# First modulation: order of the weight and table loads, and of matvecs (in halves) and weight products

## Chip, cores and metric

The kernel runs on one core of a Trainium2 chip. The metric is the device time of one execution in microseconds (us); of several executions the median is given. Engines: TensorE (PE; PEld is its load of the stationary operand), VectorE (DVE), ScalarE (ACT), GpSimd (POOL) and SyncE (SP), which here only issues DMAs.

## What is computed

The reference runs two blocks on 256 tokens of 1024 features (`x`), with a second stream of 256 tokens (`ctx`) in the first block. Only the start of the first block matters here: a modulation from a conditioning vector, then one product for queries, keys, values and more.

```
for l in range(DEPTH):
    mod_x = (silu_c @ w_mod[l] + b_mod[l])[:, None, :]
    mod_c = (silu_cc @ w_mod[l] + b_mod[l])[None, None, :]
    sh1, sc1, g1, sh2, sc2, g2 = jnp.split(mod_x, 6, axis=-1)
    ...
    px = modulate(x, sh1, sc1) @ w_in[l]      # x * (1 + sc1) + sh1
    pc = modulate(ctx, csh1, csc1) @ w_in[l]
    qx, kx, vx, ux, gbx, gcx, fx = split_proj(px)
```

Everything behind that (attention, convolution, a Fourier mix, MLPs, in the second block a state space layer and another attention) is the same work in both kernels.

## The kernel before

The program is one stream of instructions for each engine, in the order in which the Python code emits them; an engine works strictly in that order and waits on semaphores. Python generators are "lanes" of work, and each `next(lane)` emits its next piece on all the engines that it needs. Writing those calls in another order is all it takes to change the schedule.

Weights come as units of 512 rows by 512 columns (1 MB, `raw`, five buffers). `build_plan` (line 337) lists them in the order of loading; `load_upto(n)` (238) emits the loads of the first n on SyncE's queue, and `done_with` (252) lets the next one follow when a unit has been used. For a product in pieces of 128 x 1024, ScalarE casts the weights to `whi` (line 266) and VectorE subtracts to `wlo` (line 277); `gemm` (284) does three matmuls for each tile: `whi` with the high part of the data, `wlo` with the high part, `whi` with the low part (lines 306 to 308 where tokens come out on the lanes).

The stage in question begins the program:

- The conditioning vectors `crow` and a table (`const0`: identity, the matrix `sum4`, and `selq`) are loaded, turned, and become silu(c) in `cs1` (lines 438 to 521). Bias vectors and others come in rows (`vrow`) and are turned by `trans_vec` (523); rows 3 (state space parameters) and `ldr` follow at once (530 to 535).
- The modulation that the first product needs (shift and scale, 2048 columns) comes in four quarters q = 0 to 3, two units each. `gemv` (546) multiplies silu(c) with the two units of a quarter by 4 matmuls each (`gv`, line 556), VectorE transposes the result (line 562), PE sums it with `sum4` (`g`, line 566), VectorE adds the bias (line 945, with line 946: "VectorE's sums" below).
- `mod_split` (line 760 on) then makes the modulated row tiles 2 q and 2 q + 1: ScalarE the high part `mh` (line 768), VectorE the whole `m` (769) and the low part `ml` (777), for each row tile first the 256 tokens of `x` and then those of `ctx`.
- `x` and `ctx` come in two halves of features (`load_x`), turned by PE (`transpose_x`, line 930).
- The v product (lane `gv` in `first0`, 96 matmuls) takes the row tiles in four pieces; piece p needs the modulation of quarter q = p. Each `next(gv)` emits half a piece: 12 matmuls. The first half makes the tokens of `x`, the second those of `ctx`.
- The lane `flow` prepares parameters of the state space layer: steps of some twenty small VectorE operations on 128 x 32, at four places of this stage.

`first0` (line 1704) writes that order out by hand. For q = 1 to 3 it emits both halves of the matvec of quarter q with VectorE's transposition; half a piece of the v product for quarter q - 1; `g` with the sums; the other half piece; `mod_split`; a step of `flow`. The last piece (24 matmuls) and then the q and k product (lines 310 to 312) follow.

Of the kernel before, what the change touches and what calls it, by code (L numbers as in the profile page):

```python
# [51 lines left out]
def _constants():  # L52
    """Tables that depend on shapes alone: name -> [128, n]."""
# [34 lines left out]
_GROUPS = (("ident", "sum4", "selq"), ("cos", "sin", "cs64"), ("c256", "s256"), ("hd2", "selh", "mask"))  # L88
# [15 lines left out]
def program(ctx: ExitStack, tc: tile.TileContext, A, out, taps=None):  # L104
# [27 lines left out]
    class Slots:  # L132
        """[128, 256] tiles, two of them in a slot."""
# [25 lines left out]
    def weave(main, *lanes):  # L159
        """For every step of main one of each lane; the rest of the lanes follows."""  # L160
        for _ in main:
            pump()
            for f in lanes:
                next(f, None)
        for f in lanes:
            run(f)

    def mix(order, *lanes):
        """Steps of the lanes in this order, and then the rest of them, those of the first last."""
        for i in order:  # L170
            f = lanes[int(i)]
            if callable(f):
                f()
            else:
                next(f, None)
        for g in (*lanes[1:], lanes[0]):
            if g is not None and not callable(g):
                run(g)
# [19 lines left out]
    class Unit:  # L198
        """Four row tiles by 512 columns of a matrix."""
# [13 lines left out]
    class Job:  # L213
        """All of a product's weights, 1024 rows by 512 columns, in four pieces: two row tiles of all columns
        where the other operand comes piece by piece, or else four row tiles of half the columns."""
# [40 lines left out]
    def split_weights(n, need=None):  # L256
        """Of the first n pieces what float32r holds of the weights; of the first need (all but one) the rest too."""
# [26 lines left out]
    def gemm(key, *passes, tok=False, nm=4):  # L284
        """For each pass (hi, lo, n, evac): evac(i, product) for nm tiles of 128 output features (tokens if tok).
        Products of 256 columns come two at a time."""
# [36 lines left out]
    def over2(t):  # L323
        """A [128, 256] factor for two row tiles."""
        return t.rearrange("p (o n) -> p o n", o=1).to_broadcast([128, 2, 256])
# [4 lines left out]
    def parts2(t, ps):  # L330
        """For each of two products its place in t."""
# [99 lines left out]
    C = {}  # L431

    def constants(i, tag, eng):
        t = const.tile([128, max(_CW[1], _CW[3]) if i else _CW[0]], F32, name=f"cst{i}", tag=tag)
# [4 lines left out]
    SP.dma_start(crow[0:8], A["c"].rearrange("b (k p) -> (b k) p", p=128))  # L439
    S.dma_start(crow[8:16], A["c_ctx"].rearrange("(k p) -> k p", p=128))  # L440
    S.dma_start(crow[16:24], A["c_2"].rearrange("b (k p) -> (b k) p", p=128))
    constants(0, "cst0", SP)
# [56 lines left out]
    G.dma_start(lam_in, A["diff_lambda"].rearrange("(o l) f d -> o (l f d)", o=1).to_broadcast([128, 512]))  # L499
# [32 lines left out]
    V.tensor_copy(ldr, ld.rearrange("k (g o) -> k g o", o=1).to_broadcast([32, 2, 64]))  # L532
    trans_vec(3)
    dt = const.tile([128, 32], F32, name="dt")
    transposed(dt, ldr.rearrange("k g p -> k (g p)"), 32)

# [5 lines left out]
    def fourths(t, q):  # L542
        """Of every 128 columns those that belong on the lanes of quadrant q."""
        return t.rearrange("p (i c) -> p i c", c=128)[:, :, 32 * q:32 * q + 32]

    def gemv(units, out_, wait=False, halves=False):
        """out_(p8): p8[:, i, s] = silu(c, c_ctx, c_2)[s] @ w[:, 128 i : 128 i + 128], feature on the lane."""
# [23 lines left out]
    def fillers():  # L571
        """Steps, three for each of the modulations that are left to TensorE."""
# [19 lines left out]
    def gemv_lanes(groups, lag=4):  # L592
        """The same with the products summed over row tiles on a vector engine, in small steps."""
# [59 lines left out]
    def rsqrt_steps(dst, v, n):  # L653
        """dst = 1 / sqrt(v): a first guess, then a step of second and one of third order."""
# [25 lines left out]
    # x and ctx, feature on the lane, two row tiles side by side  # L680
# [4 lines left out]
    class Stats:  # L685
        """Sums over the features of XT[s] and of their squares, tokens in four quadrants."""
# [4 lines left out]
        def add(self, n=1):  # L691
            """The next n row tiles are there."""
# [34 lines left out]
        def small_ln(self):  # L727
            """Steps: 1 / deviation and -mean / deviation, both over D."""
# [34 lines left out]
    def mod_split(parts, start=False):  # L763
        """Steps: hi + lo = src * sc + sh, by lane, for each of the parts."""
# [14 lines left out]
    def mod_split2(hl, src, k, gp, sh):  # L779
        """The same for the row tiles k and k + 1, src and each of hl side by side."""  # L780
# [8 lines left out]
    class Tiles:  # L789
        """[128, 256] row tiles, two side by side in a slot."""  # L790
# [10 lines left out]
    class Course:  # L801
        """A norm in two lanes: sums, factors and quotients, and what becomes of those, by pairs of row tiles."""
# [33 lines left out]
    class Norm:  # L836
        """Layer norm of XT[s] in place; split modulated parts into the columns of hl.
        Gain and bias for XT are keep: at once, or later if there are modulated parts."""
# [35 lines left out]
    def needing(g, key, *courses):  # L874
        """The product g, a pass for each of the courses, which keep ahead of it."""
# [36 lines left out]
    def mod_of(g, b, sc, sh):  # L912
        """Gain and bias of the modulated layer norm."""
# [23 lines left out]
    def first_mod(q):  # L937
        """Steps: the modulated row tiles 2 q and 2 q + 1."""
# [8 lines left out]
        yield from gemv(mq[q], out_)  # L947
# [6 lines left out]
    def attention(l, heads, q, k, v, streams, sink):  # L954
        """Differential attention in steps; sink(h, outputs [e, tokens]) for every head."""
# [4 lines left out]
        def operands(h):  # L960
            """Steps: what float32r holds of q and k, and next to it, on the other half of the rows, what is left:
            q as it is beside its rest, k's rest beside k."""
# [130 lines left out]
    def layer(l, mh, ml, first, ns, last=None):  # L1093
        """first(evacuations): steps of the products up to q, k and v."""
# [5 lines left out]
        def rope(t, n, outs=None):  # L1100
            """For n heads side by side, in place or into outs."""
# [117 lines left out]
        def residual(stats, gate, j, tw_=tw):  # L1219
            """Evacuation of a product into XT for the columns of the streams tw_."""  # L1220
# [93 lines left out]
    def cross(order, g, courses, *lanes, streams=1):  # L1314
        """Products g and, between them, norms of what the first of them makes."""
# [89 lines left out]
    def s5_prep():  # L1405
# [32 lines left out]
        # turns of 4, 8, ... 128 tokens  # L1438
# [9 lines left out]
        # the powers 1 to 4 of a token's factor, and the factors of B and C  # L1448
# [3 lines left out]
        def times(re, im, a, b, n):  # L1452
            """re + i im = a * b, for n columns of pairs."""
# [24 lines left out]
    def over(t, p0, np_, n, lead=None):  # L1478
        """[128, np_ pairs] of a [128, 32] tile, for each of n columns (and of lead planes)."""
# [5 lines left out]
    def s5_turns():  # L1485
        """Turns of every step, and the decay of four tokens."""
# [24 lines left out]
    def turn_all(dst, src, P, Q, p0):  # L1511
        """Steps: dst = src times each of the factors; [128, n, 2, 4, 16] and [128, 2, 4, 16]."""
# [9 lines left out]
    def s5_group(a):  # L1522
        """Steps: C and B of four pairs of groups, turned by 0 to 3 tokens (C) and by 0 to 4 (B)."""
# [30 lines left out]
    def s5_prepare(a, i, mats):  # L1554
        """Steps: the factors of two pairs' matrices, apart for each group."""
# [642 lines left out]
```

## Time and profile before

| | us |
|---|---|
| three runs | 1398.65, 1407.0, 1410.64 |
| median | 1407.0 |
| span of the profiled execution, first to last instruction | 1406.5 |
| PE busy in it | 1331.4 |
| VectorE busy in it | 1017.6 |
| ScalarE busy in it | 619.4 |

The profiled execution's own time is not listed apart; its span lies 0.5 us below the median of the runs. Rows of the timeline give the start of an instruction (or of a few of the same kind in a row, x4), its duration, and in brackets how long its engine had been idle and what ended that.

### The profile page before, as it was taken

What the parts mean: (1) busy time and instruction counts of PE and PEld (TensorE: products, weight loads), DVE (VectorE), ACT (ScalarE), POOL (GpSimd) and SP (SyncE); (2) the same over time, 40 slices, a digit from 0 to 9 for tenths busy, and PEclk for the clock granted to TensorE, in tenths of its full rate; (3) what the DMA queues carried; (4) which work ended last, traced back from release to release, by engine and by line L of the source; (5) the groups of instructions that cost most, each with busy time, mean ns of one, the idle gap of its engine ahead of it and who ended that gap; (6) DMA issues with size and microseconds to landing.
All of it is one profiled execution on the core that took longest, in us unless ns stands there. A gap on an engine that the chain in (4) does not pass through costs nothing.

```text
span 1406.5 us, 23747 instructions
## 1 busy us (share of the span) xinstructions
PE 1331.4 (95%) x9118; PEld 1143.0 (81%) x9118; DVE 1017.6 (72%) x2087; ACT 619.4 (44%) x1237; POOL 281.8 (20%) x532
## 2 busy tenths in 40 slices
PE   5899999999999999999999889999989899999998
PEld 3676666997888788888877779999977799879888
DVE  4778755588977767667948877788675577777875
ACT  2424443275023140233545548667646024565552
POOL 4042100001111011110213415666430222002000
PEclk8999999999999999999999989999998689999999
DMA  9725445115566747461336455776796657544241
GB/s 332 241 76 171 165 163 194 61 61 190 200 212 236 269 150 269 153 237 61 114 120 230 135 183 167 241 242 212 246 349 238 211 200 244 210 150 155 88 150 31
DMA packets 160514, 258.69 MB, mean 184 GB/s; under 512 B 29152, under 2 KB 54064, under 8 KB 160400
## 3 DMA queue, kind: packets, MB, share of 16 engines
q1 hardware_dynamic: 138912, 233.15, 48.9%
q0 software_dynamic: 8528, 22.39, 4.5%
q10 hardware_dynamic: 12960, 1.63, 0.8%
q8 instruction: 72, 1.18, 0.3%
q14 instruction: 42, 0.34, 0.1%
HBM read 240.33 MB, written 16.81 MB: 183 GB/s over the span
## 4 chain that ended last, share of the span: by engine, by line
PE 36%; DVE 7%; ACT 3%; DMA 3%; issue 1%; SPq 0%; ACTq 0%; DVEq 0%
PE mm L310 8%; PE mm L311 8%; PE mm L312 8%; DVE wlo L277 1%; DMA ud<-u 1%; PE mm L307 1%; PE mm L308 1%; PE mm L306 1%; PE pi L1599 1%; PE bc L749 1%; DMA cn<-in_a_C_im_dram 1%; ACT s L2104 1%; PE py L1914 1%; PE py L1916 1%; PE py L1915 1%
## 5 line engine op out<-in xcount | busy, mean ns | idle before, releaser
L310 PE MATMUL mm<-mh,whi 128*128 128x256 f32 (+1 forms) x1344 | 430.4, 320 | 1.3 <-ACT r L1267 1.0
L312 PE MATMUL mm<-mh,wlo 128*128 128x256 f32 (+1 forms) x1344 | 421.3, 313 | 2.0 <-DVE wlo L277 1.9
L311 PE MATMUL mm<-ml,whi 128*128 128x256 f32 (+1 forms) x1344 | 421.0, 313 | 0.9 <-DVE ml L787 0.6
L266 ACT CAST whi<-raw 128x1024 fp32r<-128x1024 f32 x226 | 234.3, 1048 | 321.7 <-PE mm L311 251.9
L277 DVE TENSOR_TENSOR wlo<-raw,whi 128x1024 fp32r<-128x1024 f32 x256 | 309.3, 1222 | 31.0 <-ACT whi L266 28.6
L310 PEld LDWEIGHTS mm<-mh,whi 128*128 128x128 f32 x1344 | 259.5, 193 | 27.6 <-issue 10.0
L312 PEld LDWEIGHTS mm<-mh,wlo 128*128 128x128 f32 x1344 | 259.0, 193 | 17.3 <-DVE wlo L277 3.2
L311 PEld LDWEIGHTS mm<-ml,whi 128*128 128x128 f32 x1344 | 259.5, 193 | 15.2 <-DVE ml L787 1.5
L310 PE MATMUL mm<-hh,whi 128*128 128x256 f32 (+1 forms) x544 | 179.6, 330 | 0.4 <-DVE xT L1226 0.4
L312 PE MATMUL mm<-hh,wlo 128*128 128x256 f32 (+1 forms) x544 | 177.8, 327 | 1.8 <-DVE wlo L277 1.8
L311 PE MATMUL mm<-hl,whi 128*128 128x256 f32 (+1 forms) x544 | 177.7, 327 | 0.0
L268 POOL TENSOR_SCALAR whi<-raw 128x1024 fp32r<-128x1024 f32 x30 | 42.9, 1430 | 421.4 <-PE mm L311 356.6
L633 DVE SCALAR_TENSOR_TENSOR ga<-raw,ce,ga 128x512 f32<-128x512 f32 x154 | 120.1, 801 | 3.5 <-DMA raw<-in_a_mod_w_dram 1.0
L310 PEld LDWEIGHTS mm<-hh,whi 128*128 128x128 f32 x544 | 103.4, 190 | 10.9 <-issue 2.0
L312 PEld LDWEIGHTS mm<-hh,wlo 128*128 128x128 f32 x544 | 103.4, 190 | 10.9 <-DVE wlo L277 2.0
L311 PEld LDWEIGHTS mm<-hl,whi 128*128 128x128 f32 x544 | 103.4, 190 | 8.5
L1226 DVE SCALAR_TENSOR_TENSOR xT<-mm,mod_l,xT 128x256 f32<-128x256 f32 x120 | 53.8, 479 | 48.2 <-PE mm L312 48.1
L1286 DVE TENSOR_TENSOR hl<-r,hh 128x512 fp32r<-128x512 f32 x44 | 30.6, 696 | 75.8 <-ACT r L1285 75.7
L556 PE MATMUL gv<-raw,cs 128*32 128x512 f32 x352 | 51.4, 690 | 7.6 <-DMA raw<-in_w_mod_dram 4.2
L1001 ACT ACTIVATE e<-sc,mx 128x512 f32<-128x512 f32 (+1 forms) x48 | 29.4, 616 | 49.1 <-DVE mx L998 48.7
L310 PE MATMUL mm<-xh,whi 128*128 128x256 f32 (+1 forms) x160 | 49.3, 308 | 1.2 <-ACT xh L650 1.2
L312 PE MATMUL mm<-xh,wlo 128*128 128x256 f32 (+1 forms) x160 | 48.9, 305 | 0.2 <-DVE wlo L277 0.2
(411 smaller groups left out, 2121.8 us busy)
## 6 DMA issues: line engine op xcount, KB each, us to landing
raw<-in_w_mod_dram SPq DMA_DIRECT2D x40, 1024.0 KB, 5.2
raw<-in_w_up_dram SPq DMA_DIRECT2D x32, 1024.0 KB, 6.1
raw<-in_w_down_dram SPq DMA_DIRECT2D x32, 1024.0 KB, 5.9
raw<-in_w_in_dram SPq DMA_DIRECT2D x24, 512.0 KB, 4.8
raw<-in_a_mod_w_dram SPq DMA_DIRECT2D x12, 1024.0 KB, 5.5
raw<-in_b_mod_w_dram SPq DMA_DIRECT2D x12, 1024.0 KB, 12.3
raw<-in_w_mod_dram SPq DMA_DIRECT2D x16, 512.0 KB, 9.7
raw<-in_w_in_dram SPq DMA_DIRECT2D x8, 1024.0 KB, 6.9
```

Source lines behind the costliest of these rows:

```text
L266: S.copy(a, raw)
L268: G.tensor_scalar(a, raw, 1.0, 0.0, op0=MU, op1=AD)
L277: V.tensor_sub(b, raw, a)
L306: T.matmul(p, mh[k][:, c], a[:, kk, :], start=s, stop=False)
L310: T.matmul(p, a[:, kk, c], mh[k], start=s, stop=False)
L311: T.matmul(p, a[:, kk, c], ml[k], start=False, stop=False)
L312: T.matmul(p, b[:, kk, c], mh[k], start=False, stop=e)
L556: T.matmul(ps[32 * q:32 * q + 32, :], cs1[:, 4 * h + q, :], raw[:, q, :], start=(h == 0), stop=(h == 1), tile_position=(0, 32 * q))
L633: V.scalar_tensor_tensor(a, u.raw[:, j, :], f, a, op0=MU, op1=AD)
L1001: S.activation(e, ps[p], AF.Exp, bias=mx[p], scale=1.0, accum_out=sm[:, p:p + 1])
L1226: V.scalar_tensor_tensor(XT[s][r], ps[:, 256 * a:256 * a + 256] if whole else ps[a], md[s][:, gate * 8 + r:gate * 8 + r + 1], XT[s][r], op ...
L1286: V.tensor_sub(b, r, a)
```

## The change

The order of emission changes at the start of the program; the arithmetic does not.

- Loads. The first weight unit is issued on SyncE's queue before all else. `crow` and `const0`, now without `selq`, go to ScalarE's queue. `selq` is a table of its own. It, the rope table (`const1`) and the input of the lambdas go to SyncE's queue in the middle of quarter 3, instead of GpSimd's queue.
- `trans_vec(3)` and what belongs to it (`s5_vectors`) move behind the first quarter's modulation and the casts of the first weights.
- The matvec of a quarter is emitted in two halves: half a piece of the v product, four matmuls for the first unit, the other half of the piece, four for the second unit, `g`, `mod_split`. One of the four steps of `flow` in this stage, that of q = 1, moves behind it.

```diff
-_GROUPS = (("ident", "sum4", "selq"), ("cos", "sin", "cs64"), ("c256", "s256"), ("hd2", "selh", "mask"))
+_GROUPS = (("ident", "sum4"), ("cos", "sin", "cs64"), ("c256", "s256"), ("hd2", "selh", "mask"), ("selq",))
...
-    SP.dma_start(crow[0:8], A["c"].rearrange("b (k p) -> (b k) p", p=128))
+    load_upto(1)
+    S.dma_start(crow[0:8], A["c"].rearrange("b (k p) -> (b k) p", p=128))
     S.dma_start(crow[8:16], A["c_ctx"].rearrange("(k p) -> k p", p=128))
     S.dma_start(crow[16:24], A["c_2"].rearrange("b (k p) -> (b k) p", p=128))
-    constants(0, "cst0", SP)
+    constants(0, "cst0", S)
...
-    G.dma_start(lam_in, A["diff_lambda"].rearrange("(o l) f d -> o (l f d)", o=1).to_broadcast([128, 512]))
...
     trans_vec(0)
     ldr = t256("ldr", 128)[:32].rearrange("k (g p) -> k g p", g=2)
-    V.tensor_copy(ldr, ld.rearrange("k (g o) -> k g o", o=1).to_broadcast([32, 2, 64]))
-    trans_vec(3)
     dt = const.tile([128, 32], F32, name="dt")
-    transposed(dt, ldr.rearrange("k g p -> k (g p)"), 32)
+
+    def s5_vectors():
+        V.tensor_copy(ldr, ld.rearrange("k (g o) -> k g o", o=1).to_broadcast([32, 2, 64]))
+        trans_vec(3)
+        transposed(dt, ldr.rearrange("k g p -> k (g p)"), 32)
...
-        yield from gemv(mq[q], out_)
+        yield from gemv(mq[q], out_, halves=True)
...
         next(mod[0])
+        next(mod[0])
         transpose_x(0)
         run(mod[0])
         load_x(1)
         split_weights(2)
+        s5_vectors()
         next(flow)
         for q in range(1, 4):
+            next(gv)
             next(mod[q])
             next(gv)
             if q == 2:
                 transpose_x(1)
             next(mod[q])
-            next(gv)
+            if q == 3:
+                constants(1, "cst1", SP)
+                constants(4, "cst4", SP)
+                SP.dma_start(lam_in, A["diff_lambda"].rearrange("(o l) f d -> o (l f d)", o=1).to_broadcast([128, 512]))
             next(mod[q])
+            next(mod[q], None)
             if q == 2:
                 split_weights(4)
                 state["ahead"] = AHEAD
-            next(flow)
-        constants(1, "cst1", G)
+            if q > 1:
+                next(flow)
```

SyncE's queue at the start of the program. Before (`raw` are weights, `x` halves of the inputs; DMAHW0 and so on are the semaphores of earlier loads, handed out in turn):

```order
L439 DMA crow<-in_c_dram 8x128
L435 DMA cst_78<-in_const_dram 128x672
L210 DMA raw<-in_w_mod_dram 128x4x256 x2
L210 DMA raw<-in_w_mod_dram 128x4x256 [waits DMAHW0_49]
L210 DMA raw<-in_w_mod_dram 128x4x256 [waits DMAHW1_49]
L470 DMA x_90<-in_x_dram 128x512 [waits DMAHW2_49]
```

The same queue now:

```order
L210 DMA raw<-in_w_mod_dram 128x4x256 x2
L210 DMA raw<-in_w_mod_dram 128x4x256 [waits DMAHW0_49]
L210 DMA raw<-in_w_mod_dram 128x4x256 [waits DMAHW1_49]
L471 DMA x_90<-in_x_dram 128x512 [waits DMAHW2_49]
L471 DMA x_92<-in_x_dram 128x512 [waits DMAHW3_49]
```

`crow` and the table are gone from the front. The first semaphore was that of `crow`; now it is that of the first weights.

PE around the `g` of quarter 1, before (`whi_303` and `wlo_307` are the first piece's weights, `mh_190` and `mh_191` row tiles of quarter 0):

```order
L306 MATMUL mm_352<-whi_303,mh_191 128x512
L307 MATMUL mm_352<-wlo_307,mh_191 128x512
L308 MATMUL mm_352<-whi_303,ml_199 128x512
L566 MATMUL g8_359<-gsb_343,cst0_78 32x12 x4
L306 MATMUL mm_370<-whi_303,mh_190 128x512
L307 MATMUL mm_370<-wlo_307,mh_190 128x512
```

The same place now (`whi_295` is the first piece, `whi_297` and `wlo_399` the second, `mh_184` the first row tile of quarter 1):

```order
L306 MATMUL mm_356<-whi_295,mh_183 128x512
L307 MATMUL mm_356<-wlo_299,mh_183 128x512
L308 MATMUL mm_356<-whi_295,ml_191 128x512
L558 MATMUL gv_342<-raw_107,cs1_146 32x512 x4
L568 MATMUL g8_372<-gsb_370,cst0_81 32x12 x4
L306 MATMUL mm_328<-whi_297,mh_184 128x512
L307 MATMUL mm_328<-wlo_399,mh_184 128x512
```

Before, `g` stood between two halves of the first piece. Now the matvec's second half stands right ahead of it, and the second piece, on quarter 1's own row tiles, right behind it.

VectorE at the `wlo` of the second piece, before (`wlo_439`; the rows on `sc32` and `s32` are the end of a step of `flow`, `gsb_437` the transposition of quarter 2's matvec, which reads `gv_422`):

```order
L1348 TENSOR_SCALAR sc32_404<-sc32_404 128x32
L1350 TENSOR_SCALAR sc32_402<-sc32_402 128x32
L1372 CAST e32_419<-sc32_402 128x32
L1373 TENSOR_TENSOR s32_400<-sc32_404,e32_419 128x32
L562 STREAM_TRANSPOSE gsb_437<-gv_422 128x512
L277 TENSOR_TENSOR wlo_439<-raw_102,whi_305 128x1024
L945 TENSOR_TENSOR mod_l00_173<-g8_484,vT_81 128x2 x2
```

And now (`wlo_399`; `ml_192` and `ml_193` are the two row tiles of quarter 1, `gsb_471` the transposition for quarter 2):

```order
L779 TENSOR_TENSOR ml_192<-m_383,mh_184 128x256
L779 TENSOR_TENSOR ml_192<-m_384,mh_184 128x256
L771 TENSOR_SCALAR m_391<-xT01_173,sc1p0_180,mod_l00_165 128x256
L771 TENSOR_SCALAR m_392<-xT11_177,sc1p1_181,mod_l01_166 128x256
L779 TENSOR_TENSOR ml_193<-m_391,mh_185 128x256
L779 TENSOR_TENSOR ml_193<-m_392,mh_185 128x256
L277 TENSOR_TENSOR wlo_399<-raw_102,whi_297 128x1024
L564 STREAM_TRANSPOSE gsb_471<-gv_416 128x512
```

The `wlo` stood behind a step of `flow` and a transposition; it now follows the four `ml` of quarter 1, and the transposition comes after it.

## Rows read from the trace of the kernel before

**Rows 1.** The page: span, and busy time of the engines.
```profile
span 1406.5 us, 23747 instructions
...
PE 1331.4 (95%) x9118; PEld 1143.0 (81%) x9118; DVE 1017.6 (72%) x2087; ACT 619.4 (44%) x1237; POOL 281.8 (20%) x532
```
**Rows 2.** PE's waits, 10 to 67 us: for whom, us in total, times, longest.
```profile
PE gv L556 <- DMA raw<-in_w_mod_dram: 4.2, 2, 3.0
PE mm L307 <- DVE wlo L277: 3.5, 1, 3.5
...
PE g L566 <- DVE gsb L562: 2.4, 1, 2.4
```
**Rows 3.** Busy by stretch: us, PE, PEld, DVE, ACT, POOL, clock, DMA share, GB/s.
```profile
17.00:25.80 8.80, 4.64 (x31) 1.07 (x29) 7.19 (x30) 5.44 (x12) 5.58 (x12) 0.66 1.11 343
25.80:30.70 4.90, 4.90 (x16) 3.66 (x12) 0.85 (x3) 0.00 (x0) 0.00 (x0) 0.56 1.07 368
39.78:43.74 3.96, 3.96 (x11) 3.10 (x12) 0.00 (x0) 0.00 (x0) 0.00 (x0) 0.57 1.10 348
56.26:60.50 4.24, 4.24 (x20) 3.35 (x21) 4.17 (x13) 1.62 (x4) 0.00 (x0) 0.64 0.77 241
66.54:92.00 25.46, 25.46 (x115) 21.03 (x114) 18.44 (x87) 9.13 (x16) 0.97 (x2) 1.00 0.39 122
```
**Rows 4.** Timeline, 0 to 26 us: start, duration, engine, line, operation.
```profile
0.76 0.40 SPq L439 DMA_DIRECT2D crow<-in_c_dram  x1
...
1.63 2.10 SPq L210 DMA_DIRECT2D raw<-in_w_mod_dram  x4
...
10.97 0.21 DVE L532 COPY ldr<-ld 32x128 f32<-32x128 f32 x1 [3.06 <-DMA ld<-in_a_log_dt_dram]
...
11.24 0.31 PE L509 MATMUL pT<-cst,ldr 32*128 32x32 f32 x1
...
15.06 2.63 PE L930 MATMUL pT<-cst,x 128*128 128x128 f32 x16
...
21.52 1.23 DVE L277 TENSOR_TENSOR wlo<-raw,whi 128x1024 fp32r<-128x1024 f32 x1 [0.16 <-ACT whi L266]
...
23.96 1.93 PE L556 MATMUL gv<-raw,cs 128*32 128x512 f32 x8 [1.15 <-DMA raw<-in_w_mod_dram]
...
25.83 0.80 PE L306 MATMUL mm<-whi,mh 128*128 128x512 f32 x1
```
**Rows 5.** Timeline, 28 to 60 us: the chain of a quarter's modulation.
```profile
30.77 0.25 PE L566 MATMUL g<-gsb,cst 128*32 128x12 f32 x8
...
31.08 0.23 DVE L945 TENSOR_TENSOR mod_l<-g,vT 128x2 f32<-128x2 f32 x2 [4.40 <-PE g L566]
...
31.61 2.08 ACT L768 ACTIVATE mh<-xT,mod_l,sc1p 128x256 fp32r<-128x256 f32 x4 [9.18 <-DVE sc1p L946]
...
33.73 0.75 DVE L777 TENSOR_TENSOR ml<-m,mh 128x256 fp32r<-128x256 f32 x2
...
33.90 1.92 PE L556 MATMUL gv<-raw,cs 128*32 128x512 f32 x16
...
38.55 1.18 DVE L277 TENSOR_TENSOR wlo<-raw,whi 128x1024 fp32r<-128x1024 f32 x1
...
48.73 3.92 ACT L266 CAST whi<-raw 128x1024 fp32r<-128x1024 f32 x4
...
55.50 0.71 DVE L562 STREAM_TRANSPOSE gsb<-gv 128x512 f32<-128x512 f32 x1
...
56.26 0.25 PE L566 MATMUL g<-gsb,cst 128*32 128x12 f32 x8 [2.35 <-DVE gsb L562]
```
**Rows 6.** Timeline, 62 to 67 us: product matmuls at the high clock; q and k begin.
```profile
63.14 0.39 PE L306 MATMUL mm<-whi,mh 128*128 128x512 f32 x1
...
63.37 0.39 PE L307 MATMUL mm<-wlo,mh 128*128 128x512 f32 x1
...
66.54 0.39 PE L310 MATMUL mm<-mh,whi 128*128 128x512 f32 x1
```

More of the change, by code (lines that the diff above doesn't have):

```diff
@@ L433, in constants @@
     def constants(i, tag, eng):
-        t = const.tile([128, max(_CW[1], _CW[3]) if i else _CW[0]], F32, name=f"cst{i}", tag=tag)
+        t = const.tile([128, max(_CW[1], _CW[3]) if tag == "cst1" else _CW[i]], F32, name=f"cst{i}", tag=tag)
         eng.dma_start(t[:, :_CW[i]], A[f"const{i}"])
```

## Prediction

> **What bounds the kernel now.** I read the busy shares of the page first. TensorE (PE) is busy 1331.4 of 1406.5 us [rows 1], so a change in the first 70 us counts only by what it does to PE's idle time and to PE's clock there; behind that stretch the instructions are the same ones, in nearly the same order. The second view is the list of PE's waits between 10 and 67 us [rows 2]. The reader is to see three kinds: 4.2 us in two waits for modulation weights, 3.5 us in one wait for a split of weights on VectorE (`wlo`, line 277), and 2.4 us in one wait of the small sum (`g`, line 566) for VectorE's transposition of the matvec. The third view is the busy time by stretch [rows 3]. From 17 to 25.8 us the DMA engines move 343 GB/s at a share over 1, so this part goes at the pace of the loads. Afterwards they don't decide: no later wait in [rows 2] names a load. In three stretches the mean granted clock lies between its levels: 0.56, 0.57 and 0.64, where 0.5 is 1.2 GHz and 1.0 is 2.4 GHz. With c the mean clock, a share 2(1 - c) of the stretch is at the low level: 4.3 us after 25.8, 3.4 us after 39.78, 3.05 us after 56.26. Each comes behind a wait of PE. The fourth view, the timeline, gives durations and the order in which the engines hand over [rows 4 to 6].
>
> The point that I follow through is the start of the q and k product, at 66.54 us [rows 6]. It is when the v product and all four modulation quarters are done.
>
> **The change part by part.**
>
> *Loads at the start.* SyncE issued its first weights at 1.63 us behind two others, the first of them at 0.76 [rows 4]. Now weights are first: 0.87 us earlier. The 344 KB table ahead of them (128 x 672 x 4 bytes) becomes 82 KB on ScalarE's queue; 262 KB less at 343 GB/s [rows 3] is 0.76 us. Together the stream could be 1.6 us earlier. Against that, the third weight load waits for a semaphore that in the kernel before belonged to the tiny `crow` load and now belongs to the first 512 KB of weights, as the rows of SyncE's order show; this may leave a gap of up to a microsecond. The queue's rows bound it only from 0 to 1.5 us (512 KB at 343 GB/s); I take 0.4. The matvec of quarter 0 no longer queues behind the transpositions for the state space layer, but its gain ends where the transpositions of x (15.06 us, [rows 4]) wait for x, which stands behind these weights in the stream. So x and all up to the first `wlo` comes 1.2 us earlier; bounds 0.1 and 2.0.
>
> *First product.* It began at 25.83 us, behind both matvec halves of quarter 1, which waited for weights [rows 4]. Now it stands ahead of them, behind the vector table's copies. The first `wlo` ended at 21.52 + 1.23 = 22.75; 1.2 earlier is 21.55. Behind it VectorE copies `ldr` (0.21) and PE transposes it (0.31) [rows 4], since `s5_vectors` stands there in both engines' order: with the two handovers 22.2 us. That is 3.6 us earlier than 25.83. But quarter 1's two matvec halves still have to run, 0.96 us each at the high clock (1.92 for both, [rows 5]): 1.9 us. Lead: **-1.8 us** (bounds -0.8 and -3.0: the bounds of the paragraph above, and the matvecs at the low clock, 1.93 us a half, [rows 4]). Both kernels enter this product at the low clock, so that cancels.
>
> *The chain of each quarter.* This is the largest term. Before, 12 product matmuls (half a piece, 12 x 0.23 = 2.8 us, [rows 6]) stood between matvec and `g`, 12 more behind `g`, and the next matvec before the next piece. Now `g` stands right behind the second half of the matvec, and behind `g` at once the product that needs this very modulation (PE's rows of the order). Nothing on PE covers the chain. From the rows: handover 0.1 and transposition 0.71, handover 0.05 to `g`; 0.31 from `g` (30.77) to VectorE's sums (31.08); 3.40 from there to the end of the last `ml` (33.73 + 0.75 = 34.48) [rows 5]. For quarter 1 the next in VectorE's order is the `wlo` of the second piece, 1.18 to 1.23 (I take 1.22), which the piece's second matmul needs; 0.05 handover. The sum is 0.86 + 0.31 + 3.40 + 1.22 + 0.05 = 5.84 us, of which PE fills 0.4 with `g` and one matmul: **5.4 us idle**. For quarter 2 the `wlo` needs a cast by ScalarE, queued behind four `mh`: 0.53 + 2.08 + 1.0 (3.92 / 4) = 3.61 from VectorE's sums instead of 3.40 [rows 5], so **5.6 us**. For quarter 3 the `wlo` of the last piece is done already: the last product waits only for `mh` and for the `ml` of the first 256 tokens, of which the last ends 0.4 earlier: 0.86 + 0.31 + 3.0 + 0.05 = 4.2, less `g` (0.2), two table transpositions (0.3 each, as for `ldr`, [rows 4]) and five matmuls (1.15), some **2.3 us**. That is 13.3 us of new idle time. Bounds 8 and 15: the lower if quarters 1 and 2 cost 3.5 each, the longest such wait in [rows 2], and quarter 3 only 1.0.
>
> Removed are the two old waits, 3.5 and 2.4 [rows 2]: the second piece's `wlo` no longer stands behind a state space step and a transposition, and neither does quarter 3's transposition. Net **+7.4 us** (bounds +2 and +9).
>
> *Clock.* Behind the removed waits lay 3.4 + 3.05 us at the low clock [rows 3]; at half speed half of it is lost, 3.2 us. Behind the new waits, both longer, I expect two such stretches again, of nearly the length of the longest in [rows 3]: 4.2 us each, 4.2 lost, **+1.0 us**. Bounds -1, if much of them falls into the waits themselves, and +4, if there are four. The trace shows two waits of 2.35 and 3.5 us, each followed by a low stretch. The Trainium skill, "TensorE: Matmul & The Clock Gate", section "HAM oscillation — how this bites in real kernels", says that where short runs of matmuls alternate with waits each run starts throttled, and the cost is paid every time instead of once; it speaks against this order of work. By that rule quarter 3's 2.3 us would have its low stretch too, another 1.5 us, and the time would be 1415.1; [rows 3] agree for their two cases, and my sum leaves the third out.
>
> *Edits at nothing.* One of the four state space steps of this stage moves behind it, into a stretch in which VectorE is busy 18.44 of 25.46 us [rows 3]; it is about as long as the 3.5 us wait that such a step made [rows 2] and fits into the 7 that are free, and if that cover were gone they would show as waits of PE (rival C). The rope table, `selq` and the lambda inputs leave GpSimd's queue for SyncE's, behind ten half loads of 512 KB, the last of which waits for quarter 3's matvec. That ends some 9 us before the v product does (the chain of 4.2 and the 20 matmuls behind it), and the last unit with the three tables, 2 MB at 343 GB/s [rows 3], is 6 us, so they land before the v product ends; the lambdas stand on VectorE behind it, the rope later still. Weights queued behind them are for products over 20 us away. Taking 640 KB out of the saturated stretch brings x's second half and later weights up to 1.9 us sooner, which nobody waits for after 26 us. Matvecs in halves cost the same number of matmuls.
>
> **Sum.** -1.8 + 7.4 + 1.0 = +6.6 us. All of it passes on, since PE does not wait for anything but itself just behind the stage (25.46 busy of 25.46, [rows 3]). The sum is made against the span, 1406.5: 1413.1. The median of the three runs, 1407.0, lies 0.5 above the span, so the forecast is **1413.6 us**, +0.5%.
>
> **The rivals.**
>
> *A, faster.* The earlier start wins, because the chains overlap more than I grant. Place: the first matmul of each piece. The products come by pairs, a first one of `whi` and `mh`; if PE's new waits stay as long as the removed ones (5.9 us together) and short enough for the clock to stay up, the lead stands and the low stretches go: -1.8 - 3.2 = -5.0 on the median, 1402.0 us. For it: the first `mh` is there about 1.05 us after VectorE's sums begin (0.53 and 0.52, [rows 5]), so PE can start each piece long before its chain is through. Against it: VectorE works strictly in its order, and `wlo` is behind four `ml`. It decides where a quarter's chain is under 3 us. Chance 0.13.
>
> *B, absorbed.* The stage ends late, but later waits of PE that don't depend on it shrink, half of the +6.6: 1410.3 us. For it: 75 us of PE's span are idle [rows 1]. Against it: the later chains hang on PE's own products. Chance 0.12.
>
> *C, clearly slower.* VectorE's debt. At the end of the v product it still owes a state space step before the `wlo` of the second q and k piece. If that `wlo` comes after PE's first piece (24 matmuls, 5.5 us), PE waits at three pieces for some 2.4 us each, the smaller of the two waits in [rows 2], and gets one more low stretch (1.6 lost): +8.8 more, 1422.4 us. For it: both large waits of VectorE in [rows 2] arose in just this way. Against it: 7 us free in that stretch. Chance 0.13.
>
> **How the numbers follow.** The forecast has 0.62. Its own bounds add up to -2 (-3.0 + 2 - 1) and +12.2 (-0.8 + 9 + 4), that is 1405 to 1419; the rivals' times at 1402 and 1422.4 carry 0.26, so I let the range of 8 in 10 reach from 1401 to 1422. The three runs of before spread from 1398.65 to 1410.64, and 1% (14 us) is about what a measurement of this kernel can tell from no change. Faster by over 1% (below 1393) no case gives, I leave 0.04 to what I have not seen; slower by over 1% (above 1421) is most of rival C, 0.12; within 1% has 0.84.
>
> **What would show it.** Right: the first product matmul starts near 22 us, PE waits some 5 us behind the `g` of quarters 1 and 2 with VectorE's `wlo` as the last release, and the q and k product starts between 71 and 75 us. The step on loads is wrong if the transpositions of x start at 15 or later. The chain term is wrong if those two waits are under 3.5 us; the clock term if there are no low stretches behind them. The forecast as a whole fails if the q and k product starts before 67 us, or if PE waits for `wlo` after it (rival C).

## The result, and the profile after

| | before | after |
|---|---|---|
| runs | 12, from 1394.51 to 1410.64 us | 12, from 1408.87 to 1418.52 us |
| median | 1402.2 us | 1413.7 us |
| profiled execution, own time | not listed | 1415.5 us |
| its span | 1406.5 us [rows 1] | 1413.7 us |

The change made the kernel slower: the ratio is 1.0081 (95% interval 1.0057 to 1.0106), +11.4 us. The forecast time, 1413.6 us, was met. The forecast difference, +6.6 us on a median of 1407.0, was not: the median of before, over twelve runs, is 4.8 us lower than the three runs that I started from. So two things have to be explained: whether the first stage did what I said, and where the other 5 us are.

The page of after has the same work as [rows 1], and PE idle for 79 us instead of 75:

```profile
span 1413.7 us, 23764 instructions
...
PE 1334.4 (94%) x9118; PEld 1143.3 (81%) x9118; DVE 1017.1 (72%) x2087; ACT 619.9 (44%) x1237; POOL 277.6 (20%) x530
```

PE's waits between 10 and 76 us, which answer to [rows 2] (for whom, us in total, times, longest):

```profile
PE pT L509 <- DVE ldr L535: 4.9, 1, 4.9
PE mm L306 <- ACT whi L266: 3.6, 1, 3.6
PE mm L307 <- DVE wlo L277: 3.4, 2, 2.9
PE g L568 <- DVE gsb L564: 2.6, 3, 0.9
PE mm L306 <- ACT mh L770: 1.8, 2, 1.2
PE mm L308 <- DVE ml L779: 0.2, 1, 0.2
PE pT L509 <- PE g L568: 0.2, 1, 0.2
```

The 3.5 us for `wlo` and the 2.4 us for `g` are replaced by the chains of quarters 1 to 3: apart from the first row, which lies ahead of the first product, 11.8 us in ten waits. The timeline of after, against [rows 4 to 6]:

```profile
6.95 0.27 PE L509 MATMUL pT<-cst,crow 24*128 24x24 f32 x1 [6.95 <-DMA cst<-in_const_dram]
...
12.67 2.89 PE L932 MATMUL pT<-cst,x 128*128 128x128 f32 x16
...
19.39 1.22 DVE L277 TENSOR_TENSOR wlo<-raw,whi 128x1024 fp32r<-128x1024 f32 x1 [0.17 <-ACT whi L266]
...
20.89 0.28 PE L509 MATMUL pT<-cst,ldr 32*128 32x32 f32 x1 [4.91 <-DVE ldr L535]
...
21.10 0.80 PE L306 MATMUL mm<-whi,mh 128*128 128x512 f32 x1
...
26.64 0.50 PE L306 MATMUL mm<-whi,mh 128*128 128x512 f32 x1
...
26.98 0.39 PE L307 MATMUL mm<-wlo,mh 128*128 128x512 f32 x1
...
27.21 0.40 PE L308 MATMUL mm<-whi,ml 128*128 128x512 f32 x1
...
29.59 1.07 PE L558 MATMUL gv<-raw,cs 128*32 128x512 f32 x8
...
31.50 0.25 PE L568 MATMUL g<-gsb,cst 128*32 128x12 f32 x8 [0.84 <-DVE gsb L564]
31.81 0.23 DVE L947 TENSOR_TENSOR mod_l<-g,vT 128x2 f32<-128x2 f32 x2 [0.37 <-PE g L568]
...
35.12 1.22 DVE L277 TENSOR_TENSOR wlo<-raw,whi 128x1024 fp32r<-128x1024 f32 x1
...
36.40 0.80 PE L307 MATMUL mm<-wlo,mh 128*128 128x512 f32 x1 [2.90 <-DVE wlo L277]
...
53.19 0.80 PE L306 MATMUL mm<-whi,mh 128*128 128x512 f32 x1 [3.64 <-ACT whi L266]
...
54.45 0.79 PE L307 MATMUL mm<-wlo,mh 128*128 128x512 f32 x1 [0.46 <-DVE wlo L277]
...
72.90 0.39 PE L310 MATMUL mm<-mh,whi 128*128 128x512 f32 x1
```

The x transpositions start 2.4 us earlier (12.67 instead of 15.06), the first product 4.7 us earlier. Quarter 1 is seen from 29.59 to 36.40: matvec, VectorE's transposition, `g`, sums, and the `wlo` at 35.12 that PE waits for. The q and k product starts at 72.90, **6.36 us later** than at 66.54 [rows 6]. Busy time by stretch in after, against [rows 3] (us, PE, PEld, DVE, ACT, POOL, clock, DMA share, GB/s):

```profile
14.50:21.10 6.60, 1.69 (x20) 1.30 (x18) 4.86 (x17) 5.80 (x13) 5.05 (x11) 0.74 1.10 347
21.10:72.90 51.80, 39.99 (x188) 25.30 (x187) 26.43 (x104) 15.01 (x28) 1.20 (x3) 0.83 0.74 242
21.10:25.64 4.54, 4.54 (x13) 3.37 (x12) 3.09 (x17) 0.00 (x0) 1.20 (x3) 0.62 1.11 342
36.40:42.30 5.90, 5.90 (x19) 3.67 (x19) 0.00 (x0) 0.00 (x0) 0.00 (x0) 0.56 0.57 184
54.45:60.00 5.55, 5.55 (x19) 3.60 (x19) 5.04 (x19) 1.53 (x2) 0.00 (x0) 0.62 0.00 0
66.50:72.00 5.50, 5.29 (x21) 3.69 (x22) 4.99 (x23) 3.78 (x7) 0.00 (x0) 1.00 1.03 349
73.00:98.50 25.50, 25.50 (x115) 21.08 (x114) 22.49 (x110) 9.14 (x16) 1.14 (x2) 1.00 0.44 133
```

Behind each of the two large waits the clock is at 0.56 and 0.62. Behind the stage PE is busy 25.50 of 25.50 us, and VectorE 22.49 where it was 18.44: it does the moved state space step there, and nobody waits.

### The profile page after: what moved, and what is told of

Read it like the earlier page. It is cut to its first block, busy times and chain, and to the rows that moved or that the text cites. A ratio compares the mean times of both kernels' runs of the same rounds, so it can differ in the third digit from the quotient of the medians.

```text
span 1413.7 us, 23764 instructions
## 1 busy us (share of the span) xinstructions
PE 1334.4 (94%) x9118; PEld 1143.3 (81%) x9118; DVE 1017.1 (72%) x2087; ACT 619.9 (44%) x1237; POOL 277.6 (20%) x530
```

## The experiments

The kernels by the start of the q and k product ("stage end"), the mean granted clock of the first 80 us, and the time. Ratios are to the kernel before on the same chip.

| kernel | stage end | clock | median us | ratio (95%) |
|---|---|---|---|---|
| before (first profile) | 66.54 | 0.89 | 1402.2 | |
| ctl: before again | 65.52 | 0.91 | 1401.4 | 0.9984 (0.9957 to 1.0011) |
| after | 72.90 | 0.87 | 1413.7 | 1.0081 (1.0057 to 1.0106) |
| after_again | 73.66 | 0.85 | 1412.0 | 1.0062 (1.0036 to 1.0087) |
| newloads | 64.62 | 0.89 | 1401.0 | 0.9969 (0.9937 to 1.0000) |
| newloop | 73.49 | 0.89 | 1414.1 | 1.0063 (1.0039 to 1.0086) |
| flowback | 76.52 | 0.85 | 1417.6 | 1.0094 (1.0060 to 1.0128) |
| early | 66.07 | 0.91 | 1406.1 | 1.0021 (1.0000 to 1.0043) |
| vec_later | 73.38 | 0.85 | 1407.9 | one run |
| best1 | 56.89 | 0.96 | 1396.4 | 0.9941 (0.9920 to 0.9963) |
| best2 | 54.81 | 0.96 | 1398.3 | 0.9954 (0.9930 to 0.9979) |
| step_alone | 57.36 | 0.98 | 1396.0 | 0.9931 (0.9898 to 0.9964) |
| wlo_alone | 58.89 | 0.94 | 1401.3 | 0.9954 (0.9929 to 0.9979) |
| step_before | 60.04 | 0.96 | 1395.1 | 0.9929 (0.9900 to 0.9958) |

### Both kernels once more

> The kernel before, unchanged, to get a second profile of it. Theory 1 (the change costs only what the first stage shows, +6.4 us at the start of the q and k product, and the rest of the measured +11.5 us is that the profile of before that I started from was one of its longer executions): the second profile has the q and k product at 66.0 to 67.0 us again, and its span lies near 1400, with the difference to the first profile (1406.5) arising late in the program. Theory 2 (the change costs the further 5 us between 70 and 180 us, where the trace of after has low stretches of the clock): the second profile of before has no low stretch of the clock between 100 and 190 us either, as the first had none.

> The kernel after once more, to see which of its low stretches of the clock come back. Theory 1 (the clock behind the stage is chance from one execution to the next): q and k product at 72 to 74 us again, but other low stretches between 90 and 190 us than the 13.6 us of the first profile, and the mean clock over its runs equal to that of before. Theory 2 (the change lowers the clock there): three or so low stretches between 90 and 190 us again, and the mean clock over all its runs below that of before by some 0.003, which is 4 us.

Behind the stage the first two profiles differ by more than the 6.36 us: a given matmul of the product is 12.4 us later in after at 190 us, and 6.2 us later at the end. PE's waits there are the same ones; the clock is not. Four profiles follow, first the first one of before. Its first row is the stage from its first product. Each has the row on 80 to 250 us; all but the last have the one on 1000 us to the end. A row that begins with `sum` adds up the stretches at the low level from the first product to 80 us: their length, then the busy times in them (before: 25.83 to 30.1, 40.4 to 43.8 and 57.4 to 60.8 us):

```profile
25.83:66.54 40.71, 34.83 (x174) 24.71 (x171) 28.02 (x117) 15.00 (x28) 0.00 (x0) 0.86 0.84 275
sum 11.07, PE 11.07 PEld 8.61 DVE 4.15 ACT 1.92 POOL 0.00; mean PE 3.69 PEld 2.87 DVE 1.38 ACT 0.64 POOL 0.00
80.00:250.00 170.00, 161.21 (x851) 114.35 (x850) 114.24 (x273) 68.07 (x182) 25.93 (x36) 1.00 0.44 152
1000.00:1420.00 420.00, 381.22 (x2970) 350.87 (x2968) 284.99 (x521) 187.20 (x351) 51.72 (x111) 0.93 0.53 180
```

The second profile of before (ctl; low from its first product to 27 and from 37.2 to 44 us):

```profile
sum 7.98, PE 6.87 PEld 5.52 DVE 1.85 ACT 0.00 POOL 0.00; mean PE 3.44 PEld 2.76 DVE 0.93 ACT 0.00 POOL 0.00
80.00:250.00 170.00, 161.24 (x830) 113.17 (x829) 112.80 (x271) 66.98 (x181) 25.98 (x36) 0.97 0.45 152
1000.00:1420.00 420.00, 380.57 (x3010) 350.31 (x3008) 287.64 (x529) 189.33 (x356) 55.53 (x121) 0.94 0.54 182
```

The first of after (low from its first product to 24.6, from 34.8 to 41.6 and from 51.9 to 58.7 us):

```profile
sum 17.10, PE 13.75 PEld 10.15 DVE 10.55 ACT 4.08 POOL 1.20; mean PE 4.58 PEld 3.38 DVE 3.52 ACT 1.36 POOL 0.40
80.00:250.00 170.00, 161.23 (x825) 113.83 (x824) 120.19 (x321) 68.14 (x183) 25.22 (x36) 0.96 0.43 145
1000.00:1420.00 420.00, 387.09 (x3054) 356.54 (x3052) 289.77 (x537) 193.38 (x364) 59.48 (x135) 0.94 0.54 185
```

And the second of after (after_again; low from its first product to 26.6, from 33.4 to 40.2, from 50.5 to 57.3 and from 67.5 to 71 us; its last row is the end of the v product):

```profile
sum 22.90, PE 16.85 PEld 12.25 DVE 15.96 ACT 8.21 POOL 1.39; mean PE 4.21 PEld 3.06 DVE 3.99 ACT 2.05 POOL 0.35
80.00:250.00 170.00, 161.24 (x824) 113.29 (x823) 118.71 (x317) 66.67 (x181) 25.25 (x36) 0.96 0.43 147
67.00:72.00 5.00, 4.78 (x14) 3.52 (x13) 4.41 (x23) 2.25 (x4) 0.00 (x0) 0.66 0.99 345
```

With c the mean clock of a stretch, 2(1 - c) of it is at the low level. Between 80 and 250 us that is none in the first profile of before, 10.2 us in the second, 13.6 us in both of after. From 1000 us to the end it is 59 and 50 us in before, 50 in after. So one program gives or loses 5 us by the clock from one execution to the next, at places that the change does not touch. My Theory 1 was wrong in its detail (ctl's span is 1405.1, not near 1400; its q and k product starts at 65.52, not after 66.0; and the difference does not only arise late). Theory 2 falls in its first half: before does have low stretches between 100 and 190 us. Its second half stands: the mean clock over all runs is 0.9662 for after (20 runs) and 0.9693 for before (the 91 runs beside the experiments), that is some 95 and 86 us at the low level, and at most half of the difference, 4.5 us, is lost. It is at most that, because the low level also falls into waits of PE, where no matmul runs slower for it. The means of the times are 1413.2 and 1405.0.

From the first product to 80 us the `sum` rows give 17.10 and 22.90 us at the low level for after, 11.07 and 7.98 for before. Part of it falls into waits: in the first profile of after the clock is low from 34.8 and from 51.9 us on, and the waits end at 36.40 and 53.19. PE is busy for 13.75 and 16.85 us of it in after, for 11.07 and 6.87 in before: 6.3 us more on the mean, of which half, 3.2 us, is lost. So most of the clock's loss belongs to the stage. The stage as a whole ends 7.25 us later (mean of 72.90 and 73.66 less that of 66.54 and 65.52); the two ratios stand for +11.4 and +8.7 us. Whether the 1.5 to 4 us between are a further effect of the change or the spread of the clock isn't settled.

### The loads alone, the loop alone

newloads keeps the loop of before: in after, its `for q` loop with whole matvecs and a step of `flow` in each quarter. It has the late state space vectors beside the new loads; no run takes these two apart.

```diff
-        yield from gemv(mq[q], out_, halves=True)
+        yield from gemv(mq[q], out_)
...
         next(mod[0])
-        next(mod[0])
...
         for q in range(1, 4):
-            next(gv)
             next(mod[q])
             next(gv)
...
             next(mod[q])
+            next(gv)
             next(mod[q])
-            next(mod[q], None)
...
-            if q > 1:
-                next(flow)
+            next(flow)
```

newloop is the opposite: before, with the loop of after and the old loads and tables.

> Of the change only the new order of the loads and tables and the late vector transpositions; the loop with whole matvecs is that of before. If loads and loop are two separate terms, the loads are a gain: q and k product at 64 to 65 us instead of 66.5, time 1399 to 1401 (-1.5 to -3 us on the median of before). Rival: the gain at the transpositions of x (2.4 us in after) is eaten by the first state space step, which stays between the quarters; then the q and k product stays at 66.0 to 67.0 us and the time within 1 us of before.

> Of the change only the loop (matvecs in halves, small sum and product right behind them, one state space step moved behind the stage); loads and tables as before. By my terms: chains 12.0 us of new idle as measured in after, 5.9 removed, first product at 23 us instead of 25.8 with 2.1 us of matvec still to run: q and k product at 73 to 76 us, +8 to +10 us on before, and by theory 2 some 5 us more, +13 to +15. If the loads were what costs, this kernel would lie within 3 us of before.

PE's waits in newloads from its first product to the stage end:

```profile
PE mm L307 <- DVE wlo L277: 3.5, 1, 3.5
PE g L568 <- DVE gsb L564: 2.3, 1, 2.3
```

They are the two old ones, unchanged: the loop's order brings them back. The stage ends at 64.62, 0.9 us earlier than in ctl and 1.9 earlier than in the first profile of before; the time is at most 0.6% better, and may be the same. In newloop the stage ends at 73.49 and the time is that of after. The loop is the whole loss, as I had it. But the loop holds two edits, the close order (matvec halves, `g` and the product behind each other) and the moved step; they are taken apart below. Its waits (the row on `whi` holds 3.8 us ahead of the first product):

```profile
PE mm L306 <- ACT whi L266: 7.4, 2, 3.8
PE mm L307 <- DVE wlo L277: 4.1, 3, 2.9
```

With the old loads and vectors the x transpositions start at 14.19 (newloop), with the new ones at 12.67; why these 1.5 us are not seen at the stage end is the next question.

### The state space vectors behind the first half piece

In after the first `wlo` ends at 20.61, but the first product waits for `ldr` and its transposition until 21.10. vec_later moves them behind the first half piece:

```diff
         split_weights(2)
-        s5_vectors()
-        next(flow)
         for q in range(1, 4):
             next(gv)
+            if q == 1:
+                s5_vectors()
+                next(flow)
             next(mod[q])
```

> The kernel after with the state space vectors and the first state space step issued behind the first half of the first v piece instead of ahead of it. If the transposition of the step sizes (dt), standing ahead of the first product, is what ate the gain of the loads in after (first product 0.5 us behind the end of the first wlo), the first product now begins within 0.1 us of the end of the first cast and its second matmul within 0.1 us of the end of the first wlo, and the q and k product starts 0.5 to 1 us earlier than in after: 71.5 to 72.5. If not, the first product stays at 21 us.

The timeline, and the clock of the half piece:

```profile
19.13 1.23 DVE L277 TENSOR_TENSOR wlo<-raw,whi 128x1024 fp32r<-128x1024 f32 x1 [0.16 <-ACT whi L266]
...
20.41 0.80 PE L307 MATMUL mm<-wlo,mh 128*128 128x512 f32 x1 [0.76 <-DVE wlo L277]
...
25.80 1.33 PE L558 MATMUL gv<-raw,cs 128*32 128x512 f32 x8
```
```profile
20.41:25.80 5.39, 5.39 (x13) 3.87 (x14) 0.20 (x2) 0.00 (x0) 1.76 (x4) 0.50 1.11 342
```

The first half came true: the second matmul starts 0.05 us behind the end of `wlo` (20.36), 1.3 us ahead of after's. The second half did not: the stage ends at 73.38. Now all 12 matmuls run at the low clock (0.50), where after had 0.62 over the same work, and quarter 1's matvec begins at 25.80, later than after's 25.64. Two things take the head start: the half piece runs at half speed throughout and ends at 25.27, and the two transpositions that the edit moved stand between it and the matvec (0.5 us). This is one execution of each, so a single place of the clock, and one time can't be set against a median.

### The moved step put back into after

```diff
-            if q > 1:
-                next(flow)
+            next(flow)
```

> The kernel after with the state space step of quarter 1 put back into the loop. If my edit at nothing was right (VectorE has room for the step behind the stage), putting it back only delays the wlo behind it: wait of quarter 1 up from 2.9 to some 6 us, q and k product at 75.5 to 77 us, time 3 us above after (1416 to 1418). If the moved step is what costs downstream (VectorE's debt, rival C in another form), the time is back at or below after's: 1407 to 1413, and the q and k product's lag shrinks between 75 and 180 us.

```profile
PE mm L307 <- DVE wlo L277: 6.9, 2, 6.4
PE mm L306 <- ACT whi L266: 3.6, 1, 3.6
```

The wait for `wlo` in quarter 1 goes from 2.9 to 6.4 us, the stage ends 3.6 us later, the median is 3.9 us higher (the intervals overlap, so the time alone would not show it), and nothing comes back behind the stage. The edit that I costed at nothing behind the stage costs nothing there; VectorE's debt (rival C) isn't there.

flowback and newloads differ in the close order alone: same loads, same vectors, a step of `flow` in each quarter. The stage ends at 76.52 against 64.62, and the medians are 1417.6 and 1401.0 us on the same chip. So the close order by itself costs 11.9 us of the stage.

### The order on VectorE and ScalarE, with PE's order as in after

early issues the `wlo` of the second and the casts and `wlo` of the third piece ahead of the modulation:

```diff
         for q in range(1, 4):
             next(gv)
+            if q == 1:
+                split_weights(2, 2)
+            if q == 2:
+                split_weights(4, 3)
             next(mod[q])
```

> The kernel after, with the wlo of the second and of the third v piece issued before the matvec's second half, so that they no longer stand behind the modulation on VectorE and the casts no longer behind the mh on ScalarE. If the order on VectorE and ScalarE makes the new waits (my chain term), the wait for wlo in quarter 1 falls from 2.9 to under 1 us, the wait for whi in quarter 2 from 3.6 to about 1.2, q and k product at 68 to 71 us instead of 72.9, time 1408 to 1411. Rival: the modulation itself (mh, m, ml) sets the end; then the wait only moves to ml, and the time stays within 2 us of after.

```profile
PE mm L306 <- ACT mh L770: 3.0, 3, 1.2
PE g L568 <- DVE gsb L564: 2.6, 3, 0.9
```

The waits for `whi` and `wlo` are gone; some 6 of 11.8 us are left: three times 0.9 for the transposition and up to 1.2 for `mh`. The stage ends at 66.07, better than expected, since the clock holds too (0.91). So the weight splits, which two in-order engines do behind the modulation, are part of the loss: 6.8 us of the stage. They are not all of it. best1, below, has the same loads, the moved step and an early `wlo` for the second piece too, but whole matvecs with products around `g`. Its stage ends 9.2 us before that of early (56.89), and its median is 9.7 us lower on the same chip (the intervals of the ratios are apart). Its one large wait is 1.4 us for the transposition, where early has the 6 us, and from its first product to 80 us the clock is low for 0.3 us, where early has 11.3. So of 16.0 us between after and best1 the weight splits account for 6.8, and the close order, with nothing on PE to cover the chain, for the rest.

### Versions that beat both

best1 is newloads with the step of quarter 1 behind the stage and an earlier `wlo`; best2 moves quarter 2's step too; step_alone and wlo_alone are best1 with one of its two edits; step_before is the kernel before with the moved step alone.

```diff
             next(mod[q])
             next(gv)
+            if q == 1:
+                split_weights(2, 2)
...
-            next(flow)
+            if q > 1:
+                next(flow)
```

> The loads of the change with the loop of before, the state space step of quarter 1 moved behind the stage, and the wlo of the second piece issued ahead of the small sum. Theory: of the change only the moved step and the earlier loads are good, and the loop's close order costs; the one wait of 3.5 us goes, with the low stretch of the clock behind it, so the q and k product starts at 58 to 61 us (64.6 in the run with the new loads alone), time 1394 to 1397 with the clock elsewhere as usual. Rival: the moved step comes back as waits of PE behind the stage; then the lead is gone by 190 us and the time is 1399 to 1402.

> As best1, and the state space step of quarter 2 moved behind the stage too. The wait of 2.3 us for VectorE's transposition in quarter 3 goes as well: q and k product at 55 to 58 us, time 1390 to 1395. Rival: two steps are more than VectorE has free behind the stage (25.5 us with 18.4 busy in before, 22.5 in after), so PE waits there for wlo, and the time is no better than that of best1.

> best1 without its earlier wlo: the new loads, the loop of before, and the state space step of quarter 1 moved behind the stage. If that step is what made the wait of 3.5 us, the wlo follows the transposition of quarter 2's matvec at once: a wait of 1.5 to 2 us is left, q and k product at 59 to 63 us, time 1397 to 1400. If instead the wlo's place decides, the wait stays over 3 us and the q and k product near 64.6.

> best1 with the state space step of quarter 1 left in the loop: the new loads, the loop of before, and the earlier wlo. The second piece no longer waits for wlo, but the step delays VectorE's transposition for quarter 2 by some 2 us, which the 12 matmuls before the small sum cover (2.8 us). So nearly all of best1's gain is here: q and k product at 57 to 59 us, time 1395 to 1398. Rival: the step's delay moves on to the next wait of VectorE (the transposition of quarter 3), 1 to 3 us longer: 1398 to 1401.

> The kernel before with one edit: the state space step of quarter 1 moved behind the stage. If this step alone makes the wait of 3.5 us (as the chain of before says), the wait falls to 1.5 us as in the run of the step with the new loads, and the low stretch behind it goes: q and k product at 59 to 62 us, time 1397 to 1401. If the new loads were needed for it, the q and k product stays at 64 us or later and the time within 3 us of before.

PE's waits in step_before from its first product to the stage end:

```profile
PE mm L307 <- DVE wlo L277: 1.5, 1, 1.5
PE g L566 <- DVE gsb L562: 1.4, 1, 1.4
```

The one edit takes 2.0 us from the wait for `wlo` and 1.0 from that for `g`, the clock of the first 80 us rises to 0.96, the stage ends 6.5 us earlier than in the first profile of before, and the time falls by 0.7% (0.4 to 1.0%, some 6 to 14 us). So the change held a gain and a larger loss: step_alone, which differs from after in the close order alone, ends the stage 15.5 us earlier, with ratios of 0.9931 and 1.0081. The fastest versions, step_before, step_alone and best1, can't be told apart. The earlier `wlo` alone takes the wait of 3.5 us away as well, but leaves 2.3 for `g` in quarter 3, and gains 0.5%, near what its rival said. best2 ends the stage 2.1 us before best1 and has no better time, with no wait for `wlo` behind the stage; its rival's reason isn't seen either.

## Why the prediction was right in the time and wrong in the difference

- **Base.** "The sum is made against the span, 1406.5". That execution, and the three runs, were on the long side: the kernel before has medians from 1401.4 to 1406.4 in six groups of 10 to 33 runs. The base was 4.8 us too high for the group that the result is taken against. This made the time come out right with too small a difference: that the time was met is luck.
- **Lead.** -1.8 forecast. First product -4.73, less two matvec halves of 1.07: -2.6. The x transpositions came 2.4 us earlier than in the first profile of before, but 1.8 than in ctl (14.45), within my bound of 2.0; `ldr` took back 0.5, as written. The reason was in part another than I gave. I granted the earlier matvec of quarter 0 no gain, because I had the transpositions wait for x; in [rows 4] they wait for nothing, they follow that matvec. It starts at 8.87 instead of 11.48. In before PE waited 3.2 us ahead of it for the rows that `trans_vec(3)` turns (the row below); in after these come later. How much of the lead is theirs and how much the earlier weights', no run separates. Nor is the gap that I feared between the weight loads settled: from 8 to 10 us the loads run at 280 GB/s in after, at 332 in after_again and at 348 in before, and behind that, from 14.5 to 21.1 us, at 347.

```profile
PE pT L509 <- DMA vrow<-in_ln_b_dram: 3.2, 1, 3.2
```

- **Chains.** 5.4, 5.6 and 2.3 forecast; measured 0.84 + 1.24 + 2.90 = 5.0, 0.93 + 3.64 + 0.46 = 5.0, and 1.8 for the third: 11.8 of new idle, 5.9 removed, +5.9 for +7.4. The rows of the stage confirm it without the waits: 51.80 less 39.99 idle in after, 40.71 less 34.83 in before.
- **Clock.** +1.0 in the sum. In the first pair of profiles the low stretches from the first product on grew from 10.8 to 12.9 us, +1.05: as forecast. Over two profiles each, the stage loses 3.2 us from its first product on, over all runs the program at most 4.5: inside my bounds, but three times the term. **This is the term that was mis-sized**: I took it from two stretches behind two waits. Behind quarter 3's waits (1.8 us in all) the clock is 0.66 in after_again (67 to 72 us), and 1.00 in the first profile of after (66.5 to 72 us). The Trainium skill, "TensorE: Matmul & The Clock Gate", section "HAM oscillation — how this bites in real kernels", tells of a kernel in which every run of matmuls behind a wait starts throttled; its waits are longer than quarter 3's, so that it would hold there was my reading, and the traces bear it out in one of two profiles.
- **What the sum left out.** -2.6 + 5.9 + 1.05 is 4.4; the stage ended 6.36 later. PE's busy time grew by 39.99 - 34.83 = 5.16, of which the matvec of quarter 1 (2.14) and the clock (1.05) are 3.2. Some 2 us are left. Part is the changeover: behind a matvec half the first product matmul holds PE 0.34 us (26.64 to 26.98), the next 0.23, and a half takes 1.07 where I took 0.96; before has such ends and starts too, with halves and waits there are more. I had costed the halves at nothing. With the clock's 3.2 us of two profiles each, some 1 us of the 7.25 is left; its cause stays open.
- **Edits at nothing.** Right for the moved step (flowback), not for the halves (above).
- **Rivals.** A's condition, chains under 3 us, is what early comes near to, and it gains 6 to 8 us on after by it. B did not come. C's wait for `wlo` behind the stage is in no profile.

## What to carry to other kernels

Read what stands ahead of the operand that PE waits for, on the engine that makes it: one step of some 3.5 us moved out of that queue took away 3.0 us of waits and was worth some 10 us (6 to 14), and much of the low clock of the stage went with them. An order in which a chain follows its matvec at once needs other work on PE between them; taking the weight splits out of the chain's queues gave back 6.8 of 16.0 us. Where a change holds several edits, run each alone: here one gained and one lost more, and the sum hid it. Before a forecast of half a per cent, take the base from many runs and the clock from more than one profile.

## What the runs showed of the hardware

- The 91 runs of the kernel before went from 1394.8 to 1414.9 us, with a mean granted clock between 0.979 and 0.961, and their low stretches moved between stages that the program never changed (80 to 250 us: 1.00 and 0.97).
- A shorter wait is worth more than its length and an earlier start less, by the clock: step_before loses 3.0 us of waits and ends its stage 5.5 to 6.5 us earlier (against the two profiles of before); vec_later starts its second product matmul 1.3 us earlier and ends the half piece 0.4 us earlier, since all of it runs at 0.50 (one execution each).
- The table with the identity, cut to a quarter and put on ScalarE's queue, reached PE's first transposition at 6.95 us instead of 4.36 (the kernel before, and 4.67 in ctl). It was issued at 2.07 us instead of 1.22, so the later issue is 0.85 us of that; from issue to use it took 4.9 us instead of 3.1, with weights on the way ahead of it. The Trainium skill, "DMA: Bandwidth & Descriptors", section "Issuing engines are not separate DMA queues", says that transfers of all issuing engines run on the same 16 DMA engines; the row agrees with that but does not prove it.
